# Two DeepNorm layers on one core: the ring of split weights becomes one tile whose four slots start at different distances from multiples of 256 bytes

## The chip, the cores and the metric

The kernel runs on one core of a Trainium2 chip. The metric is the time of one execution on the device, in microseconds (us): lower is better. Before the change it is 847.92 us, the median of 3 runs (846.06 to 848.54).

## The reference, cut to what matters

All arrays are float32; 256 tokens of width 1024 go through two layers. Each layer is a mixer of three branches, fed by one input projection, and a SwiGLU feed-forward part, each followed by a residual and a LayerNorm:

```
for l in range(DEPTH):
    mix = hybrid_mixer(x, w_in[l], attn_sinks[l], conv_w[l], w_branch_a[l], w_branch_b[l], w_branch_c[l], w_out[l])
    x = layer_norm(ALPHA * x + mix, ln1_g[l], ln1_b[l])
    ffn = swiglu(x, w_ffn_gate[l], w_ffn_up[l], w_ffn_down[l])
    x = layer_norm(ALPHA * x + ffn, ln2_g[l], ln2_b[l])
```

The mixer is sliding-window attention with sinks, a gated short convolution, and block attention. Their outputs go through a branch weight each, are gated by a sigmoid and summed, and go through `w_out`. Nearly all arithmetic is in the products of activations with weights.

## The kernel before, in words

**Split operands.** A product is not done in one pass. Every weight block and every activation is split into a high part (rounded to the type fp32r, on ScalarE) and a low part (the float32 value minus the high part, on VectorE), and three matmuls are summed: high by high, high by low, low by high. Where the weights are the stationary operand (lines 366 to 369, `trio`), two matmuls in a row load the same high weights and the third loads the low ones:

```
mm(acc, wh, src[:, 0, :], first, False)
mm(acc, wh, src[:, 1, :], False, False)
mm(acc, wl, src[:, 0, :], False, last)
```

In the helper `tokens` (lines 359 to 364) it is the other way round: the activations are stationary and the weights stream. All these matmuls are issued by line 252, so that in the profile they share that line and are told apart by their tiles: `acc`, `gc`, `br` (stationary weights, 256 columns streamed), `hp` (streamed weights, 256 columns), `pr` and `cv` (streamed weights, 512 columns, in the last projection also 256).

**Pieces, staging and the ring.** The weights come as 140 pieces of 128 x 2048 float32, 70 for each layer, the first of them inside the array `first`. A piece is loaded into one of three `raw` buffers by a DMA from SyncE's queue, split in two chunks of 1024 columns (lines 177 to 181: ScalarE writes `wh`, VectorE writes `wl`), used by TensorE, and dropped. The split parts of a piece lie in a slot. There are four slots (RING), and each has a high and a low tile of 8 KB per partition from a pool of their own (line 122, `wts`; line 172). A few pieces around the feed-forward part go instead into the places `wA` and `wB`, which share memory with other tiles. The tiles of split weights and activations all start at multiples of 256 bytes.

**Addresses of the activations.** The tile `xx` (the layer's input, split) and the tile `y` (the branches' inputs) begin with 48 unused floats (AHEAD, lines 299 and 646), so that every operand read from them starts 192 bytes past a multiple of 256; the tiles `rest` fill the line up. The feed-forward's hidden activations (`hidA`, `hidB`) and the merged branches (`mx`) start at multiples of 256. All blocks of weights and activations that a matmul reads are 512 or 1024 bytes long or apart, so the distance between the starts of its two operands, counted modulo 256 bytes, is the same for all matmuls of one kind.

**What sets the order.** The program is written in a fixed order for TensorE, VectorE, ScalarE and SyncE (line 126). The class `Plan` (lines 53 to 101) keeps estimated times of the engines, and the splits and evictions are put in the order that it finds; `open_splits` (line 159) starts a piece's split as soon as a slot has been dropped. These estimates know nothing of addresses. Between the long streams of matmuls stand small ones: transposes (`tp`, line 265), attention scores (`s`) and attention outputs (`yp`, lines 484 and 486).

Of the kernel before, what the change touches and what calls it, by code (L numbers as in the profile page):

```python
# [10 lines left out]
FR = mybir.dt.float32r  # L11
# [5 lines left out]
P = 128  # L17
# [7 lines left out]
PIECE = 2048  # L25
CHUNK = 1024
RING = 4
# [6 lines left out]
FAR = 1.0e30  # L34
LINE = 64
EARLY = 7
AHEAD = 48


# [77 lines left out]
def trunk(ctx: ExitStack, tc: tile.TileContext, x, first, w, sinks, conv, ln, out):  # L117
    nc = tc.nc
    pool = lambda name, bufs, **k: ctx.enter_context(tc.tile_pool(name=name, bufs=bufs, **k))
    const = pool("const", 1)  # L120
    raws = pool("raws", RAWS)
    wts = pool("wts", RING)
    keep = pool("keep", 1)
    work = pool("work", 2)
    ps = pool("ps", 4, space=bass.MemoryType.PSUM)
    ctx.enter_context(tc.manual_schedule(engines={ENG.PE, ENG.DVE, ENG.Activation, ENG.SP}))
# [8 lines left out]
    total = L * PER_LAYER  # L135
    slots = [0.0] * RING
    spare, ready, chunks, raw, landed, rawfree = {}, {}, {}, {}, {}, {}
    pos = {"load": 0, "split": 0, "take": 0}

    def cut(j):  # L140
# [3 lines left out]
    def load():  # L144
        j = pos["load"]
        if j >= total:
            return
        pos["load"] += 1
        if j:
            raw[j] = raws.tile([P, PIECE], FT, name="raw")  # L150
            for s in cut(j):
                nc.sync.dma_start(raw[j][:, s], w[j - 1][:, s])
        landed[j] = max(landed.get(j - 1, 3.5), rawfree.get(j - RAWS, 0.0) + 2.0) + 3.0
        open_splits()
# [4 lines left out]
    def open_splits():  # L159
        while pos["split"] < pos["load"]:  # L160
            j = pos["split"]
            if j in place:
                if place[j] not in spare:
                    return
                t = spare.pop(place[j])
                both = keep.tile([P, 2, PIECE], FR, tag=place[j], name="w" + place[j])
                ready[j] = both[:, 0, :], both[:, 1, :]
            else:
                if not slots:
                    return  # L170
                t = slots.pop(0)
                ready[j] = wts.tile([P, PIECE], FR, name="wh"), wts.tile([P, PIECE], FR, name="wl")
            pos["split"] += 1
            if j:
                split_piece(j, max(t, landed[j]))
# [7 lines left out]
    def split_piece(j, t, n=CHUNK):  # L183
        def last(task):
            rawfree[j] = task.ready
            load()

        need = T.pe + 5.2 * (j - pos["take"])
        ss = [slice(c, c + n) for c in range(0, PIECE, n)]
        chunks[j] = [T.add(parts(j, s), t - (1.5 if len(cut(j)) > 1 and not i else 0.0), max(need - t, 0.0) + 0.001 * i, last if s.stop == PIECE else None)  # L190
                     for i, s in enumerate(ss)]

    def take():
        j = pos["take"]
        pos["take"] += 1
        T.run()
        T.finish(*chunks.pop(j))
        return j

    def drop(j):  # L200
        if j in place:
            if j % PER_LAYER == N_IN + N_BR + N_OUT:
                spare["B"] = T.pe
        else:
            slots.append(T.pe)
        del ready[j]
        open_splits()
# [90 lines left out]

    xx = keep.tile([P, AHEAD + KD * 2 * S], FR, name="xx")
    xx = xx[:, AHEAD:].rearrange("p (k a s) -> p k a s", k=KD, a=2)  # L300
    xk = [xx[:, k] for k in range(KD)]
    rest = keep.tile([P, LINE - AHEAD], FT, name="rest")
    nc.gpsimd.memset(rest, 0.0)

    both = keep.tile([P, KD, 2 * S], FT, tag="A", name="first")
    rest = keep.tile([P, LINE - AHEAD], FT, name="rest2")
    nc.gpsimd.memset(rest, 0.0)
# [12 lines left out]
    spin = ps.tile([P, P], FT, tag="o", name="spin")  # L320
    for i in range(EARLY):
        nc.tensor.matmul(spin, idle, idle, start=True, stop=True)
# [289 lines left out]
    def mixer_tiles():  # L612
        mix = keep.tile([P, 18 * S + 4 * (S + 2) + 56], FT, tag="mix", name="mix")
        aq, ak, av, cq, ck, cv = [
            mix[:, lo * S:hi * S].rearrange("p (k s) -> p k s", k=k)
            for lo, hi, k in ((0, 4, 4), (4, 5, 1), (5, 6, 2), (6, 10, 4), (10, 14, 4), (14, 18, 2))]
        return aq, ak[:, 0, :], av, cq, ck, cv, mix[:, 18 * S:18 * S + 4 * (S + 2)].rearrange("p (k s) -> p k s", k=4)
# [26 lines left out]
    for l in range(L):  # L644
        aq, ak, av, cq, ck, cv, up = tiles = mix or mixer_tiles()
        y = keep.tile([P, AHEAD + 12 * 2 * S], FR, tag="A", name="y")
        y = y[:, AHEAD:].rearrange("p (b k a s) -> p b k a s", b=3, k=4, a=2)
        nc.gpsimd.memset(up[:, :, 0:2], 0.0)
# [39 lines left out]
        for n in range(2):  # L688
            j = take()
# [120 lines left out]
        merge()  # L810
        spare["A"] = spare["B"] = T.pe
        open_splits()

        hid, last_f = [], {f: [] for f in range(NF)}
# [127 lines left out]
```

## Time and profile before

| what | value |
|---|---|
| median of 3 runs | 847.92 us (846.06 to 848.54) |
| the profiled execution: time, span | 849.0 us, 847.2 us |
| TensorE matmul busy, share of the span | 833.2 us, 98% |
| TensorE weight loads busy | 793.3 us, 94% |
| VectorE, ScalarE, GpSimd busy | 582.7, 456.0, 56.8 us |
| mean granted TensorE clock | 0.996 |
| read from HBM | 153.11 MB, 182 GB/s over the span |

The profile is of one execution. The span runs from its first to its last instruction, and the execution's own time is 1.8 us longer. A matmul's busy time overlaps that of the next, so what a matmul costs in a stream is read from a row of the chain that ended last: its length divided by its number of matmuls. That chain is followed back from the last instruction; a row of it gives start, length, engine, tile written, line and the number of instructions.

### The profile page before, as it was taken

How to read it: one execution, taken by the hardware profiler on the slowest of the kernel's cores; microseconds unless marked ns; L12 is line 12 of the kernel's file. 1: busy time of each engine (PE TensorE's matmuls, PEld its weight loads, DVE VectorE, ACT ScalarE, POOL GpSimd, SP SyncE). 2: the span in 40 equal slices, each digit the busy share in tenths (PEclk: the TensorE clock that was granted, in tenths of full speed). 3: DMA queues.
4: the chain of work that ended last, by engine and by line, in shares of the span. 5: the costliest groups of instructions: out<-in, count | busy, mean ns of one | idle time of the engine just before them, and what ended most of it. 6: DMA issues, size and time to landing. Idle time of an engine off the chain costs nothing.

```text
span 847.2 us, 15506 instructions
## 1 busy us (share of the span) xinstructions
PE 833.2 (98%) x6388; PEld 793.3 (94%) x6388; DVE 582.7 (69%) x978; ACT 456.0 (54%) x809; POOL 56.8 (7%) x81
## 2 busy tenths in 40 slices
PE   7999999999999999999999999999999999999996
PEld 6989999999899999988899899999998999999885
DVE  4688999576967566545657799966688666556435
ACT  5667687645525445434347776865563345444320
POOL 2002500000110000000000044000000100000000
PEclk9999999999999999999999999999999999999999
DMA  8843445555655555556336424554646465545511
GB/s 298 298 167 133 149 154 202 192 200 199 249 199 200 178 176 194 199 190 232 126 106 244 149 100 140 210 205 169 222 165 243 169 226 195 198 172 182 195 50 50
DMA packets 23462, 155.15 MB, mean 183 GB/s; under 512 B 2624, under 2 KB 2912, under 8 KB 5984
## 3 DMA queue, kind: packets, MB, share of 16 engines
q1 hardware_dynamic: 21888, 149.17, 49.9%
q0 software_dynamic: 1216, 4.22, 1.5%
q8 instruction: 50, 0.82, 0.4%
q10 hardware_dynamic: 288, 0.79, 0.3%
q14 instruction: 20, 0.16, 0.1%
HBM read 153.11 MB, written 1.05 MB: 182 GB/s over the span
## 4 chain that ended last, share of the span: by engine, by line
PE 96%; DMA 2%; DVE 1%; ACT 0%; issue 0%; POOLq 0%; POOL 0%; SPq 0%; DVEq 0%
PE acc L252 47%; PE pr L252 17%; PE hp L252 9%; PE br L252 8%; PE gc L252 5%; PE cv L252 3%; PE tp L265 2%; PE s L252 2%; DMA gb<-ln 1%; PE yp L484 1%; DMA first<-first 1%; PE yp L486 0%; DVE xtok L512 0%; DVE wA L181 0%; POOLq L938 0%
## 5 line engine op out<-in xcount | busy, mean ns | idle before, releaser
L252 PE MATMUL acc<-xx,wh 128*128 128x256 f32 x2304 | 405.9, 280 | 4.5 <-ACT wh L270 4.5
L181 DVE TENSOR_TENSOR wl<-raw,wh 128x1024 fp32r<-128x1024 f32 x266 | 322.3, 1229 | 110.1 <-ACT wh L180 109.5
L180 ACT ACTIVATE wh<-raw 128x1024 fp32r<-128x1024 f32 x266 | 274.0, 1053 | 191.9 <-PE acc L252 79.7
L252 PEld LDWEIGHTS acc<-xx,wh 128*128 128x128 f32 x2304 | 351.2, 189 | 5.6 <-ACT wh L270 5.0
L252 PE MATMUL acc<-xx,wl 128*128 128x256 f32 x1152 | 322.1, 280 | 0.2 <-DVE wl L271 0.2
L252 PEld LDWEIGHTS acc<-xx,wl 128*128 128x128 f32 x1152 | 219.3, 190 | 0.6 <-DVE wl L271 0.4
L252 PE MATMUL hp<-wh,xx 128*128 128x256 f32 x384 | 70.4, 281 | 0.0
L277 DVE TENSOR_TENSOR g<-g,acc 128x256 f32<-128x256 f32 x72 | 30.1, 418 | 57.6 <-PE acc L252 57.1
L252 PE MATMUL br<-y,wh 128*128 128x256 f32 x384 | 67.9, 281 | 0.0
L252 PE MATMUL pr<-wh,hidA 128*128 128x512 f32 (+1 forms) x216 | 60.7, 366 | 0.0
L252 PEld LDWEIGHTS hp<-wh,xx 128*128 128x128 f32 x384 | 59.5, 188 | 0.0
L252 PEld LDWEIGHTS br<-y,wh 128*128 128x128 f32 x384 | 58.9, 190 | 0.0
L252 PE MATMUL br<-y,wl 128*128 128x256 f32 x192 | 54.0, 281 | 0.0
L252 PE MATMUL hp<-wl,xx 128*128 128x256 f32 x192 | 53.5, 279 | 0.0
L252 PE MATMUL gc<-xx,wh 128*128 128x256 f32 x256 | 45.3, 281 | 0.0
L252 PEld LDWEIGHTS pr<-wh,hidA 128*128 128x128 f32 x216 | 39.1, 189 | 6.6
L252 PE MATMUL pr<-wh,hidB 128*128 128x512 f32 (+1 forms) x144 | 41.8, 366 | 0.0
L252 PE MATMUL pr<-wl,hidA 128*128 128x512 f32 (+1 forms) x108 | 39.5, 366 | 0.0
L252 PEld LDWEIGHTS gc<-xx,wh 128*128 128x128 f32 x256 | 39.3, 190 | 0.0
L252 PEld LDWEIGHTS hp<-wl,xx 128*128 128x128 f32 x192 | 36.1, 188 | 0.0
L252 PEld LDWEIGHTS br<-y,wl 128*128 128x128 f32 x192 | 36.0, 188 | 0.0
L252 PE MATMUL gc<-xx,wl 128*128 128x256 f32 x128 | 36.0, 281 | 0.0
(133 smaller groups left out, 957.8 us busy)
## 6 DMA issues: line engine op xcount, KB each, us to landing
raw<-w SPq DMA_DIRECT2D x136, 1024.0 KB, 5.0
gb<-ln POOLq DMA_DIRECT2D x8, 512.0 KB, 5.1
raw<-w SPq DMA_DIRECT2D x6, 512.0 KB, 11.3
first<-first SPq DMA_DIRECT2D x2, 512.0 KB, 9.2
xtok<-x SPq DMA_DIRECT2D x2, 512.0 KB, 6.2
out<-xtok SPq DMA_DIRECT2D x3, 256.0 KB, 2.0
first<-first ACTq DMA_DIRECT2D x1, 512.0 KB, 8.6
first<-first ACTq DMA_DIRECT2D x1, 256.0 KB, 4.6
```

The source lines that it names most:

```text
L180: return [act(n) + (lambda: nc.scalar.activation(wh[:, s], raw[j][:, s], AF.Copy),), dve(n) + (lambda: nc.vector.tensor_sub(wl[:, s], raw[ ...
L181: dve(n) + (lambda: nc.vector.tensor_sub(wl[:, s], raw[j][:, s], wh[:, s].bitcast(FT)),)]
L252: nc.tensor.matmul(acc, a, b, start=start, stop=stop)
L265: nc.tensor.transpose(tp[:, i, :], src(i), ident)
L277: return [dve(n) + (lambda: nc.vector.tensor_mul(dst, a, b),)]
L484: nc.tensor.matmul(yp[los[a], :], v[:, 0, vsel[a]], pts[a][:, 0:2, :], start=True, stop=False)
```

## The change

The pool of the ring is gone. One tile `ring` of 16448 floats per partition is taken as the first tile of the pool `keep`, and a slot is a pair of slices of it: the high part of 2048 floats, right behind it the low part. The four slots start at the floats 8, 4112, 8224 and 12344, that is 32, 64 and 128 bytes past and 32 bytes short of a multiple of 256 bytes (the tile itself starts at a multiple). Slots are used in turn. The tile is 256 bytes larger than the eight tiles were, so `xx`, `y` and all else behind it move by 256 bytes and stay where they were modulo 256. The distance between the starts of a matmul's two operands, weights minus activations modulo 256, was 64 bytes for `xx` and `y`; it is now 96, 128, 192 and 32 in the four slots. For `hidA`, `hidB` and `mx` it was 0 and is now 32, 64, 128 and 224. `wA` and `wB` stay as they were.

```
+SLOTS = (8, 4112, 8224, 12344)
+SLOTS_END = 16448
...
-    wts = pool("wts", RING)
     keep = pool("keep", 1)
+    ring = keep.tile([P, SLOTS_END], FR, name="ring")
...
+    turns = [0]
...
-                ready[j] = wts.tile([P, PIECE], FR, name="wh"), wts.tile([P, PIECE], FR, name="wl")
+                ready[j] = [ring[:, lo:lo + PIECE] for lo in (SLOTS[turns[0] % RING], SLOTS[turns[0] % RING] + PIECE)]
+                turns[0] += 1
```

No compute instruction changes its place on any engine. What changes is a part of the waits. A tile of a pool is given out again when everything that read it is done; of a slice, only the readers of the same bytes are waited for. On VectorE, before, in the first projections (`raw` a loaded piece, `wl` and `wh` its low and high part, the names in brackets the semaphores waited for: DMAHW a load, PE a matmul, Activation ScalarE):

```order
L181 TENSOR_TENSOR wl<-raw,wh 128x1024 [waits DMAHW3_49,PE_49,Activation_49]
L181 TENSOR_TENSOR wl<-raw,wh 128x1024 [waits Activation_49]
L181 TENSOR_TENSOR wl<-raw,wh 128x1024 [waits DMAHW4_49,PE_49,Activation_49]
L181 TENSOR_TENSOR wl<-raw,wh 128x1024 [waits Activation_49]
L181 TENSOR_TENSOR wl<-raw,wh 128x1024 [waits DMAHW5_49,Activation_49]
L181 TENSOR_TENSOR wl<-raw,wh 128x1024 [waits Activation_49]
```

The same place on VectorE in the changed kernel, where both parts lie in the tile `ring`:

```order
L186 TENSOR_TENSOR ring<-raw,ring 128x1024 [waits DMAHW3_49,PE_49,Activation_49]
L186 TENSOR_TENSOR ring<-raw,ring 128x1024 [waits PE_49,Activation_49]
L186 TENSOR_TENSOR ring<-raw,ring 128x1024 [waits DMAHW4_49,PE_49,Activation_49]
L186 TENSOR_TENSOR ring<-raw,ring 128x1024 [waits PE_49,Activation_49]
L186 TENSOR_TENSOR ring<-raw,ring 128x1024 [waits DMAHW5_49,Activation_49]
L186 TENSOR_TENSOR ring<-raw,ring 128x1024 [waits Activation_49]
```

No row moved. The wait for TensorE, which stood whole ahead of a piece's first chunk, is now one for the first half of the slot's old content ahead of the first chunk and one for the second half ahead of the second.

## The prediction

> **What bounds the kernel now.** I read the page first: the busy times, the chain by engine, and the costliest groups.
>
> ```profile
> PE 833.2 (98%) x6388; PEld 793.3 (94%) x6388; DVE 582.7 (69%) x978; ACT 456.0 (54%) x809; POOL 56.8 (7%) x81
> PE 96%; DMA 2%; DVE 1%; ACT 0%; issue 0%; POOLq 0%; POOL 0%; SPq 0%; DVEq 0%
> L252 PE MATMUL acc<-xx,wh 128*128 128x256 f32 x2304 | 405.9, 280 | 4.5 <-ACT wh L270 4.5
> L181 DVE TENSOR_TENSOR wl<-raw,wh 128x1024 fp32r<-128x1024 f32 x266 | 322.3, 1229 | 110.1 <-ACT wh L180 109.5
> L180 ACT ACTIVATE wh<-raw 128x1024 fp32r<-128x1024 f32 x266 | 274.0, 1053 | 191.9 <-PE acc L252 79.7
> L252 PE MATMUL acc<-xx,wl 128*128 128x256 f32 x1152 | 322.1, 280 | 0.2 <-DVE wl L271 0.2
> ```
>
> TensorE makes up 96% of the chain. In the largest groups it waits 4.5 us for the first split (line 270, at the start) and 0.2 us for line 271; it never waits for a split of the ring (lines 180 and 181). Those splits wait for each other and for TensorE. So neither loads nor splits bound the kernel. What counts is how fast TensorE takes one matmul after another.
>
> That is not one number. The second view is the chain in order of time (start, length, engine, tile, line, number of matmuls), here its rows of 36 or more 256-column matmuls in the first layer up to the feed-forward part, with two short ones, and the feed-forward part and the last projection of that layer:
>
> ```profile
> 11.66 11.18 PE acc L252 x82
> 22.84 8.17 PE hp L252 x72
> 35.81 10.90 PE acc L252 x96
> 47.41 4.09 PE acc L252 x36
> 64.88 5.47 PE acc L252 x48
> 74.09 8.18 PE acc L252 x72
> 86.01 9.54 PE acc L252 x84
> 100.65 9.54 PE acc L252 x84
> 114.59 8.18 PE acc L252 x72
> 127.87 8.18 PE acc L252 x72
> 139.79 9.54 PE acc L252 x84
> 152.16 5.85 PE acc L252 x48
> 158.01 33.92 PE br L252 x288
> 191.93 22.61 PE gc L252 x192
> 237.24 8.48 PE hp L252 x72
> 249.65 2.83 PE hp L252 x24
> 252.70 5.66 PE hp L252 x48
> 258.57 2.83 PE hp L252 x24
> 261.40 4.10 PE acc L252 x36
> 265.72 97.52 PE acc L252 x828
> 363.24 57.12 PE pr L252 x252
> ```
>
> Divide length by count. 8.18 / 72, 9.54 / 84 and 10.90 / 96 give 113.6 ns for one matmul; 33.92 / 288, 22.61 / 192, 97.52 / 828 and 8.48 / 72 give 117.8. These are the same matmuls, of the same shape, at the same distance of 64 bytes between their two operands, under a granted clock of 1.00 in both places (last view below). So there are two paces, and a stream that has begun in one keeps it: 828 matmuls stay at 117.8, although other engines come and go beside them. What changes the pace is a break: after the scores and transposes of the attention the stream comes back at 113.6, after the break at 152 us at 117.8, and after the two transposes ahead of 261.40 at 113.9 for 36 matmuls, only to go on at 117.8 after the next two. I read this as two streams of reads, the one of the moving operand and the one of the next weights, that stand to each other in one of two phases.
>
> There is a third pace. The end of the last projection in the timeline (start, length, engine), where `hidB` and the weights both begin at multiples of 256 bytes:
>
> ```profile
> 837.24 0.28 PE L252 MATMUL pr<-wh,hidB 128*128 128x256 f32 x1
> 837.36 0.88 PE L252 MATMUL pr<-wB,hidB 128*128 128x256 f32 x6
> 838.08 0.28 PE L252 MATMUL pr<-wh,hidB 128*128 128x256 f32 x1
> ```
>
> From 837.36 to 838.08 there are 6 matmuls: 120 ns each, at distance 0. So the addresses do have a part in it.
>
> **The change, part by part.** First, how many matmuls it touches. The groups of 256 columns on the page:
>
> ```profile
> L252 PE MATMUL hp<-wh,xx 128*128 128x256 f32 x384 | 70.4, 281 | 0.0
> L252 PE MATMUL br<-y,wh 128*128 128x256 f32 x384 | 67.9, 281 | 0.0
> L252 PE MATMUL br<-y,wl 128*128 128x256 f32 x192 | 54.0, 281 | 0.0
> L252 PE MATMUL hp<-wl,xx 128*128 128x256 f32 x192 | 53.5, 279 | 0.0
> L252 PE MATMUL gc<-xx,wh 128*128 128x256 f32 x256 | 45.3, 281 | 0.0
> L252 PE MATMUL gc<-xx,wl 128*128 128x256 f32 x128 | 36.0, 281 | 0.0
> ```
>
> With the two `acc` groups they are 2304 + 1152 + 384 + 384 + 192 + 192 + 256 + 128 = 4992. The rows at 117.8 hold 48 + 288 + 192 + 72 + 24 + 48 + 24 + 828 = 1524 in the first layer (the 48 at 152 us carry a restart in their length, and go on into the 288). The second layer has the same program; I take twice that, 3048 slow matmuls, and 4992 - 3048 = 1944 at 113.6. The mean is (3048 x 117.8 + 1944 x 113.6) / 4992 = 116.2 ns, and the difference of the paces is 4.2 ns.
>
> (a) The distances. The change does not take the two paces away by anything that the trace shows. It does change, at every piece, the distance at which the two streams run: a piece is 48 matmuls, and its successor lies in another slot. So the pace is set anew about every 5.6 us and cannot be carried through 828 matmuls. What it is set to, no row shows for distances of 32, 96 and 128 bytes; at 192 none either, as weights minus activations. Bounds: all 4992 at 113.6 is 3048 x 4.2 = 12.8 us less; all at the 120 of distance 0 is 4992 x 3.8 = 19.0 us more. Between them I take what breaks have done so far. Of the rows above with at least 36 matmuls, those that begin after a break, twelve run at 113.6 to 114 (82, 72, 96, 36, 48, 72, 84, 84, 72, 72, 84 and the 36 at 261.40; the first, with 136, still contains waits of the start, and I count it with its neighbours) and four at 117.8 (48 at 152 us, 72, 48, 828). The 24s are left out, as two transposes part them and they are hardly new beginnings. One new start in four is slow: 4992 / 4 = 1248 slow matmuls in place of 3048, and 1800 x 4.2 = 7.6 us less.
>
> (b) The 512-column matmuls. 57.12 / 252 is 226.7 ns each at distance 0. `cv` at distance 64 is the other row there is:
>
> ```profile
> 51.51 5.49 PE cv L252 x24
> ```
>
> 5.49 / 24 is 228.8. The four projections hold some 800 of them; if all went from the one to the other, it would be 800 x 2.1 = 1.7 us more, and as much less is the bound on the other side. I take nothing, and keep 1.7 both ways.
>
> (c) The finer waits. The first chunk of a piece may be written when half of the slot's old matmuls are done, 24 x 117.8 ns = 2.8 us earlier than now. TensorE waits for no ring split, so this buys nothing; what hides it is the slack of the splits. The added waits on VectorE (one ahead of a second chunk) let nothing through later than before, since TensorE's progress was waited for at the first chunk already. Nothing queued behind them comes later. Cost 0.
>
> (d) ScalarE and VectorE write to starts that are not multiples of 64 bytes in two of the slots. No row shows such a write; below, it cannot gain anything, as both are off the chain. Above: two chunks of a piece take VectorE 2 x 1229 = 2.5 us in a piece's 48 x 117.8 = 5.7 us. In the busiest long stretch, by windows,
>
> ```profile
> 262.00:363.00 101.00, 101.00 (x861) 101.00 (x861) 62.69 (x92) 48.41 (x72) 0.00 (x0) 1.00 0.57 196
> 32.00:152.00 120.00, 119.98 (x998) 113.88 (x996) 100.84 (x219) 87.94 (x207) 19.10 (x20) 1.00 0.50 178
> ```
>
> (columns: PE, PEld, VectorE, ScalarE, GpSimd busy, clock, DMA share, GB/s) VectorE is busy 62.7 of 101 us in the feed-forward part, and 100.8 of 120 in the mixer, which is the place where its cover is thin: 19 us in 120. All of its work there would have to be a fifth slower to matter. Cost 0.
>
> The sum: 7.6 us less. The profiled execution took 849.0 us and would take 841.4. The median of the runs lies 1.1 us below that execution, so I give 847.9 - 7.6 = **840.3 us**.
>
> **The rivals.**
>
> *All fast.* The new distances stay clear of each other and every stream runs at 113.6: 12.8 us less, with the 512-column matmuls perhaps 1.7 more off: 835.1, down to 833.4. For it: a pace of 113.6 is held for 96 matmuls in a row, so it is a steady one. Against it: four different distances would all have to be good.
>
> *Nothing.* The pace is a matter of when the streams start, and addresses only matter at distance 0. A change of slot inside an unbroken stream is then no new start, the 3048 stay slow, and the time stays at 847.9. For it: 828 matmuls pass 17 changes of slot without a change of pace (though all at equal distance). Against it: 120 beside 117.8. The Trainium skill speaks for this rival: its page "SBUF — State Buffer", section "Who interferes with whom", gives TensorE two independent read ports, one for the moving operand and one for the weights, and says that it never waits on anyone. By it all matmuls of one shape would run alike wherever they read; the trace has 113.6, 117.8 and 120, so I give it little.
>
> *Slower.* The new distances include 32 and 96 bytes, which are odd multiples of 32, and 32 is the nearest to 0, the worst that the trace shows. If the two slots that lie 32 bytes off a multiple of 64 run at 120, and the other two as forecast (three in four fast, 114.65), the mean is (120 + 114.65) / 2 = 117.3 against 116.2 now: 4992 x 1.1 = 5.5 us more, 853.4. With all four at 120 it is 866.9. It decides as soon as the mean pace is over 116.2 ns; two slots at 118.5 with two others at 114 still break even. For it: distance 0 has no fast pace at all in the trace. Against it: 64 has.
>
> **How the numbers follow.** A measurement of this kernel can tell about 0.3% from no change: 2.5 us, so faster means below 845.4 and slower above 850.5. Chances: the forecast, one start in four slow, 0.36, of which 0.03 falls within 0.3%; all fast 0.24; nothing 0.12; slower 0.28. Faster is 0.33 + 0.24 = 0.57, the same 0.15, slower 0.28. The range reaches from all fast with a little beyond (833.4, less some 2 us for `hidB`'s 120 and for the rough count: 831) to the slower case with two slots at 120 and the 512-column matmuls against it (853.4 + 1.7, and a part of the way to 866.9: 858). What is left out is the far end of the slower case and a gain beyond the fast pace, under 0.2 together. The forecast's own range is 836 to 845.
>
> **What would show it right or wrong.** Right: in the chain the feed-forward rows of 828 matmuls take about 95 us in place of 97.5, and in the timeline the pace changes from slot to slot, with stretches of 113.6 inside that row; the waits of TensorE stay as they are. All fast: 94.1 us for these 828 and 32.7 for the 288 `br`. Nothing: 97.5 again. Slower: over 98 us there, with paces of 120 and more in single pieces, and rows of the mixer that were at 113.6 above 115. Wrong in another way: waits of TensorE for `ring` at lines 185 and 186, or chunks that take longer than 1229 and 1053 ns by so much that they make it wait.

## The result, and the profile after

The changed kernel takes 857.33 us (median; 856.41 to 857.52, 4 runs) against 847.21 us before (the three runs above and a fourth): a ratio of 1.0118, with a 95% interval of 1.0104 to 1.0132. It is slower, where I had forecast faster.

TensorE is busy with matmuls for 843.4 of the 855.0 us. From the page of the changed kernel, in lines that the prediction showed of the kernel before (`ring` now stands for `wh` and `wl`):

```profile
L257 PE MATMUL acc<-xx,ring 128*128 128x256 f32 x3456 | 418.7, 281 | 2.4 <-ACT ring L275 2.2
L186 DVE TENSOR_TENSOR ring<-raw,ring 128x1024 fp32r<-128x1024 f32 x266 | 322.7, 1229 | 93.2 <-ACT ring L185 92.2
L185 ACT ACTIVATE ring<-raw 128x1024 fp32r<-128x1024 f32 x266 | 274.9, 1054 | 104.6 <-PE pr L257 52.2
```

TensorE waits 2.4 us for the first split (line 275, at the start; it was 4.5, at line 270) and for none at lines 185 and 186, and a chunk takes 1229 ns on VectorE and 1054 on ScalarE, against 1229 and 1053. So neither the waits nor the odd starts of the writes have a part in it. Some rows of the chain in order of time, changed kernel (start, length, engine, tile, line, number):

```profile
33.23 11.43 PE acc L257 x96
72.65 8.50 PE acc L257 x72
84.93 9.96 PE acc L257 x84
152.67 5.85 PE acc L257 x48
...
266.96 97.82 PE acc L257 x828
364.78 58.42 PE pr L257 x252
426.84 8.53 PE hp L257 x72
453.21 11.38 PE acc L257 x96
572.63 5.89 PE acc L257 x48
688.18 97.87 PE acc L257 x828
786.05 61.45 PE pr L257 x330
```

The mixer's rows have lost their fast pace: 8.50 / 72 and 9.96 / 84 are 118.1 and 118.6 ns where 113.6 stood. The rows that were slow got no faster: 97.82 / 828 is 118.1. For the accounting, the same places of the second layer in the chain of the kernel before:

```profile
423.97 8.48 PE hp L252 x72
450.32 10.90 PE acc L252 x96
566.67 5.85 PE acc L252 x48
681.27 97.52 PE acc L252 x828
778.79 60.90 PE pr L252 x330
```

From the row of 96 to the row of 48 the mixer took 116.35 us in either layer (35.81 to 152.16, 450.32 to 566.67) and takes 119.44 and 119.42: 6.2 us more. From there to the 828, 113.56 and 114.60 have become 114.29 and 115.55: 1.7 more. The two rows of 828: 0.3 more each. From the 512-column matmuls of the first feed-forward part to `hp`, 60.73 has become 62.06, 1.3 more, and from those of the second to the end of the span 68.4 has become 69.0, 0.5 more. Together 10.3 us. The start (up to the row of 96) came 2.6 us earlier in this execution, 33.23 against 35.81, so the span grew by 7.8 only, from 847.2 to 855.0. The medians differ by 10.1, as the accounting without the start does.

What each slot costs is read from a view by windows that begin and end with a piece, here four pieces of 48 matmuls in the feed-forward part, in the slots with distances 96, 128, 192 and 32 (window, length, then PE busy; the counts include the neighbours' matmuls at both edges):

```profile
268.21:273.85 5.63, 5.63 (x50) 5.63 (x49) 3.50 (x5) 2.82 (x5) 0.00 (x0) 1.00 0.79 242
273.85:279.55 5.70, 5.70 (x50) 5.70 (x49) 3.50 (x5) 2.70 (x4) 0.00 (x0) 1.00 0.58 198
279.55:285.20 5.65, 5.65 (x50) 5.65 (x49) 3.50 (x5) 2.70 (x4) 0.00 (x0) 1.00 0.51 178
285.20:290.88 5.68, 5.68 (x50) 5.68 (x49) 3.51 (x5) 2.71 (x4) 0.00 (x0) 1.00 0.57 186
```

Divided by 48, the lengths are 117.3, 118.8, 117.7 and 118.3 ns. The pace does change from piece to piece, as I had said, but none of the four is fast.

### The profile page after: what moved, and what is told of

It reads as the page before. It is cut to its first block, busy times and chain, and to the rows that moved or that the text cites. A ratio compares the mean times of both kernels' runs of the same rounds, so it can differ in the third digit from the quotient of the medians.

```text
span 855.0 us, 15528 instructions
## 1 busy us (share of the span) xinstructions
PE 843.4 (99%) x6388; PEld 800.7 (94%) x6388; DVE 585.9 (69%) x978; ACT 458.3 (54%) x809; POOL 56.9 (7%) x81
## 4 chain that ended last, share of the span: by engine, by line
PE 96%; DMA 2%; DVE 1%; ACT 0%; issue 0%; POOLq 0%; SPq 0%; POOL 0%; DVEq 0%
PE acc L257 47%; PE pr L257 18%; PE hp L257 9%; PE br L257 8%; PE gc L257 5%; PE cv L257 3%; PE tp L270 2%; PE s L257 2%; DMA gb<-ln 1%; PE yp L489 1%; DMA first<-first 1%; PE yp L491 0%; DVE xtok L517 0%; DVE wA L186 0%; POOLq L943 0%
## 5 line engine op out<-in xcount | busy, mean ns | idle before, releaser
L257 PE MATMUL acc<-xx,ring 128*128 128x256 f32 x3456 | 418.7, 281 | 2.4 <-ACT ring L275 2.2
L257 PEld LDWEIGHTS acc<-xx,ring 128*128 128x128 f32 x3456 | 412.1, 188 | 4.3 <-ACT ring L275 2.7
L186 DVE TENSOR_TENSOR ring<-raw,ring 128x1024 fp32r<-128x1024 f32 x266 | 322.7, 1229 | 93.2 <-ACT ring L185 92.2
L185 ACT ACTIVATE ring<-raw 128x1024 fp32r<-128x1024 f32 x266 | 274.9, 1054 | 104.6 <-PE pr L257 52.2
L257 PE MATMUL hp<-ring,xx 128*128 128x256 f32 x576 | 70.8, 282 | 0.0
L257 PEld LDWEIGHTS hp<-ring,xx 128*128 128x128 f32 x576 | 68.7, 188 | 0.1
L257 PE MATMUL br<-y,ring 128*128 128x256 f32 x576 | 68.4, 281 | 0.0
L257 PEld LDWEIGHTS br<-y,ring 128*128 128x128 f32 x576 | 68.2, 188 | 0.0
L257 PE MATMUL pr<-ring,hidA 128*128 128x512 f32 (+1 forms) x324 | 67.1, 368 | 0.0
L257 PEld LDWEIGHTS pr<-ring,hidA 128*128 128x128 f32 x324 | 55.8, 188 | 11.0
```

The lines of the kernel that those rows point to most:

```text
L185: return [act(n) + (lambda: nc.scalar.activation(wh[:, s], raw[j][:, s], AF.Copy),), dve(n) + (lambda: nc.vector.tensor_sub(wl[:, s], raw[ ...
L186: dve(n) + (lambda: nc.vector.tensor_sub(wl[:, s], raw[j][:, s], wh[:, s].bitcast(FT)),)]
L257: nc.tensor.matmul(acc, a, b, start=start, stop=stop)
```

## The experiments

**The theories.** A: each distance between the two operands has paces of its own, and 96, 128 and 32 bytes have no fast one. B: the change of distance inside a stream breaks the fast phase, whatever the distances. C: the one tile and its other waits cost the time. A further question is whether the two paces at one distance really are two phases, and whether a break chooses between them.

**All slots at multiples of 256 (u000).** One tile, but the old distances.

```
-SLOTS = (8, 4112, 8224, 12344)
+SLOTS = (0, 4096, 8192, 12288)
```

> The ring is one tile as in the changed kernel, but all four slots start at multiples of 256 bytes, so that every distance is that of the kernel before. Theory A (each distance between weights and activations has paces of its own, and only at 64 bytes is 113.4 ns one of them): 847 us, the 828 matmuls of the feed-forward part at 117.8 ns, mixer rows at 113.6. Theory B (the change of distance from slot to slot breaks the fast phase, whatever the distances): 847 us as well, since nothing changes from slot to slot. Theory C (one tile in place of eight, with its other waits, costs the time): 857 us.

847.27 us, ratio to the kernel before 1.0003 (0.9993 to 1.0014). Here and below a ratio is to executions of the kernel before that were taken beside the run (medians of 846.3 to 846.8 us). From its chain:

```profile
137.62 9.54 PE acc L257 x84
263.55 97.52 PE acc L257 x828
```

Both rows have the length of before, to the hundredth. Theory C falls.

**All slots at one distance: 128 (u064), 192 (u128), 96 (u032), 32 (u224), 0 (u192), 160 (u096).** The same edit, with all four slots 64, 128, 32, 224, 192 or 96 bytes past a multiple of 256, for example u064:

```
+SLOTS = (16, 4112, 8208, 12304)
```

> All four slots 64 bytes past a multiple of 256: distance 128 to the split activations everywhere, no change from slot to slot. In the changed kernel stationary weights at this distance took 118.7 ns on average. Theory A: 118.7 everywhere with 256 columns, also in the mixer: some 860 us. Theory B: the stream finds a steady phase and the mixer is back at 113.6 ns: 848 us or less.

> All four slots 128 bytes past: distance 192 everywhere. In the changed kernel stationary weights took 117.8 ns there and streamed weights (hp) 114.0. Theory A: 117.8 in all streams with stationary weights, 114 in hp, 512-column matmuls at 232 to 233: about 855 us. Theory B: mixer rows at 113.6, hp at 113.4 as well: 843 to 848 us.

> All four slots 32 bytes past: distance 96 everywhere. In the changed kernel stationary weights took 118.2 ns there, streamed weights 119.9, 512-column matmuls 233 to 234. Theory A: these numbers everywhere, about 861 us. Theory B: mixer rows at 113.6 again, 848 us or less.

> All four slots 32 bytes short of a multiple of 256: distance 32 everywhere, the last of the changed kernel's four. There stationary weights took 118.3 ns at it. Distances with paces of their own: 118.3 or more in all streams, no row at 113.6, 512-column matmuls at 233: 858 to 861 us. A change from slot to slot to blame: mixer rows at 113.6, 848 us.

> All four slots 192 bytes past a multiple of 256, as the activations are: distance 0 for them. If distance decides, 120.0 ns with stationary weights in every stream (as the last projection's 256-column matmuls on hidB at distance 0 in the kernel before), and 227 ns for the 512 columns of cv: some 866 us. If the multiple of 256 made the 120 there, something else.

> All four slots 96 bytes past a multiple of 256: distance 160 everywhere, untried so far. What the other runs have shown: with stationary weights a fast pace of 113.4 ns exists at 64 and 192, the odd multiples of 64; 0, 32, 96 and 128 have none. If that holds as a rule, 160 has none either: 118 to 119 ns in every stream and 857 to 862 us. If the fast pace is a matter of being far from 0, as 160 is, mixer rows at 113.4 and 850 us or less.

From the chains, a row of the mixer and the row of 828 of each; first distance 128 (u064):

```profile
141.94 10.08 PE acc L257 x84
270.09 98.25 PE acc L257 x828
```

Distance 192 (u128), with a row of the second layer:

```profile
140.73 9.89 PE acc L257 x84
266.99 97.52 PE acc L257 x828
452.62 10.89 PE acc L257 x96
```

Distance 96 (u032):

```profile
141.37 9.97 PE acc L257 x84
268.51 99.36 PE acc L257 x828
```

Distance 32 (u224):

```profile
142.05 9.94 PE acc L257 x84
269.41 97.98 PE acc L257 x828
```

Distance 0 (u192):

```profile
142.09 10.07 PE acc L257 x84
270.73 99.35 PE acc L257 x828
```

Distance 160 (u096):

```profile
141.87 10.07 PE acc L257 x84
270.29 99.36 PE acc L257 x828
```

| distance | time, us | ratio to before (95%) | ns in the mixer row | ns in the row of 828 |
|---|---|---|---|---|
| 0 | 865.47 (one run) | | 119.9 | 120.0 |
| 32 | 858.10 | 1.0142 (1.0124 to 1.0160) | 118.3 | 118.3 |
| 64 (u000) | 847.27 | 1.0003 (0.9993 to 1.0014) | 113.6 | 117.8 |
| 96 | 859.94 | 1.0159 (1.0138 to 1.0180) | 118.7 | 120.0 |
| 128 | 860.72 | 1.0170 (1.0150 to 1.0190) | 120.0 | 118.7 |
| 160 | 865.88 | 1.0227 (1.0210 to 1.0244) | 119.9 | 120.0 |
| 192 | 853.08 | 1.0074 (1.0052 to 1.0097) | 117.7 | 117.8 |

No slot changes its distance in these kernels, and still 0, 32, 96, 128 and 160 have no row at 113.6 (u128's other rows of 72 and 84 are as slow as the one shown, but its 10.89 / 96 is 113.4: at 192 the fast pace exists). Theory B would have given 848 in each. The changed kernel's 857.33 lies among its four distances' 859.94, 860.72, 853.08 and 858.10, whose mean is 857.96. Theory A stands. For 160 I had expected 857 to 862 us and 118 to 119 ns; no fast pace came, as expected, but the rows are at 119.9 and 120.0, as slow as at distance 0.

**Everything moved by 64 bytes (both64).** Slots 64 bytes past a multiple of 256, activations at a multiple.

```
-SLOTS = (8, 4112, 8224, 12344)
+SLOTS = (16, 4112, 8208, 12304)
...
-AHEAD = 48
+AHEAD = 0
```

> One tile, all four slots 64 bytes past a multiple of 256, and the unused floats ahead of xx and y taken away, so that these start at a multiple of 256: every operand has moved by 64 bytes, and the distance is 64 again. If the distance decides: mixer rows at 113.6 ns and the 828 matmuls of the feed-forward part at 117.8 as in the kernel before, some 847 to 850 us (the 512-column matmuls on hidA, hidB and mx go from distance 0 to 64, 227 to 229.5 ns, and the few pieces in wA and wB from 64 to 0). If the slots' own place in the memory decides: the paces of the run with all slots at 64 bytes, 118.7 to 120 ns, some 860 us.

842.84 us, ratio 0.9963 (0.9950 to 0.9976). From its chain:

```profile
112.54 8.18 PE acc L257 x72
125.83 8.48 PE acc L257 x72
264.64 93.88 PE acc L257 x828
```

The fast pace is back (8.18 / 72 is 113.6), in slots whose place alone had given 120. And at distance 64 there are rows at 113.6 with the operands in either place (u000, both64). So it is the distance that decides, not the place. It is also faster than I expected: 93.88 / 828 is 113.4, the whole feed-forward part of the first layer in the fast pace, while a row of the mixer (8.48 / 72) has gone over to the slow one. The same distance, the same breaks, but other phases after them; some matmuls ahead of the breaks did have another distance than before (those with `wA` and `wB`, and those on `hidA`, `hidB` and `mx`), but no run shows that this is why.

**A scan of breaks (kickscan).** The kernel before, with transposes of the identity, read by nobody, put between blocks of the feed-forward part.

```
+KICKS = ({6: 1, 8: 2, 10: 3, 12: 4, 14: 5, 16: 6}, {6: 6, 8: 5, 10: 4, 12: 3, 14: 2, 16: 1})
...
+    def kick(n):
+        for lo in range(0, n, 3):
+            tp, _ = bank([P, 3, P], "o", "kick")
+            for i in range(min(3, n - lo)):
+                nc.tensor.transpose(tp[:, i, :], ident, ident)
...
         for f in range(4, NF):
+            kick((KICKS[l]).get(f, 0))
```

> The kernel before, all at distance 64, with breaks put into the feed-forward part: 1 to 6 transposes of the identity, that nobody reads, ahead of every second block from the seventh on (1, 2, 3, 4, 5, 6 in the first layer, 6 to 1 in the second). If the two paces are two phases of the same stream, the pace after a break is a matter of its length: some of the 96-matmul stretches behind the breaks run at 113.4 ns and some at 117.8, each steadily up to the next break. If the pace belongs to the stage (other engines, data, the weights' loads), all of them stay at 117.8. The breaks cost 42 transposes of 109 ns, 4.6 us, and a start each; the time itself is no matter.

One run took 847.52 us. The chain of its first layer's feed-forward part from the 2 transposes on, and behind it two stretches of the second layer, after 4 and after 2:

```profile
282.96 11.31 PE acc L253 x96
294.27 0.33 PE kick L274 x3
294.60 10.90 PE acc L253 x96
305.50 0.44 PE kick L274 x4
305.94 11.31 PE acc L253 x96
317.25 0.55 PE kick L274 x5
317.79 10.90 PE acc L253 x96
328.69 0.66 PE kick L274 x6
329.35 33.93 PE acc L253 x288
...
711.24 10.90 PE acc L253 x96
733.60 10.92 PE acc L253 x96
```

10.90 / 96 is 113.5 and 11.31 / 96 is 117.8. After 2 transposes slow, after 3 fast, after 4 slow, after 5 fast, after 6 slow, each until the next break; the instructions of VectorE and ScalarE come in the order of the kernel before. In the second layer, with the numbers in reverse, it is slow after 6 and fast after 5, and then stays fast after 4, 3, 2 and 1 (10.90 and 10.92 above). So the pace does not belong to the stage or to the other engines. It is a state that a stream keeps and that a break can turn over; to which side, the number of transposes does not say, not even together with the pace ahead of them: 4 after a fast stretch led to slow in the first layer and left the second fast. What else counts is open. I went on with 5, which led from slow to fast both times.

**Breaks where the slow streams begin (kick5, and after_kick5 on the changed kernel).** `kick(5)` at two places of each layer:

```
+        kick(5)
         for b in range(3):
             branch(b)
...
         for f in range(4, NF):
+            if f == 5:
+                kick(5)
```

> The kernel before (distance 64) with a break of 5 transposes of the identity, read by nobody, at two places of each layer: ahead of the first branch, and ahead of the sixth block of the feed-forward part. In the scan of breaks 5 transposes led from 117.8 to 113.4 ns both times. If the phase theory holds at these places: 780 matmuls of the feed-forward part (3.4 us) and the 480 of branches and last gate (2.1 us) run at 113.4 in each layer, 11 us less, against some 3 us for the breaks: 838 to 839 us. If the phase after a break cannot be steered like this: no row changes its pace, and the breaks make it 849 us.

> The changed kernel with the same breaks at the same places. If the distances 96, 128 and 32 have no fast phase, no break can lead into one: the rows keep their 118 ns, and the breaks add 3 us: 860 us. If the changed kernel merely came out of its breaks in bad phases, the 828 and 480 matmuls get faster here too, and it takes 849 us or so.

kick5 takes 837.29 us, ratio 0.9894 (0.9872 to 0.9916). Its feed-forward part in the chain:

```profile
266.57 0.55 PE kick L273 x5
267.11 92.49 PE acc L252 x816
```

92.49 / 816 is 113.3, so the whole part now runs in the fast pace, 816 matmuls that took 117.8 each before. The branches behind the other break did the same: 32.66 / 288 is 113.4 in the chain, where 33.92 / 288 stood. after_kick5 takes 858.80 us, ratio 1.0143 (1.0125 to 1.0162), more than the 1.0118 without breaks. The same part of its chain:

```profile
270.34 96.47 PE acc L257 x816
```

96.47 / 816 is 118.2. These breaks found no fast phase to lead into, as theory A has it.

**Two distances that both have a fast pace, in turn (alt).**

```
-SLOTS = (8, 4112, 8224, 12344)
+SLOTS = (0, 4128, 8192, 12320)
```

> One tile, slots at 0, 128, 0 and 128 bytes past multiples of 256: the distance changes at every piece between 64 and 192, which alone have shown a pace of 113.4 ns with stationary weights. If a change of distance inside a stream does no harm by itself: rows of the mixer at 113.6 remain, and the time lies between the two uniform kernels or below, 845 to 853 us. If the change from slot to slot breaks the fast phase by itself: no row of the mixer below 116 ns, 855 us or more.

840.57 us, ratio 0.9928 (0.9913 to 0.9944), better than I had expected and better than either distance alone (847.27 and 853.08). The rows of 828 and of `br` in its chain:

```profile
157.32 32.85 PE br L257 x288
263.58 93.91 PE acc L257 x828
675.73 94.12 PE acc L257 x828
```

93.91 / 828 is 113.4, 94.12 / 828 is 113.7 and 32.85 / 288 is 114.1. With the same breaks ahead of them, the uniform kernels at 64 and 192 both had 97.52 there. Where the pace turns over is seen by windows over single pieces. In the second layer's 828, the piece of 48 that begins 12 matmuls in, at distance 192, and the next, at 64:

```profile
677.11:682.76 5.65, 5.65 (x50) 5.65 (x49) 3.50 (x5) 2.84 (x5) 0.00 (x0) 1.00 0.81 252
682.76:688.20 5.44, 5.44 (x50) 5.44 (x49) 3.51 (x5) 2.71 (x4) 0.00 (x0) 1.00 0.52 184
```

That is 117.7 and 113.3 ns, without a break between them, and all pieces behind them keep the 113.3. In the first layer the 12 matmuls ahead of the first change, at distance 192, take 117.6, and from the next piece on, at 64, it is fast. So a change of slot can lead a slow stream into the fast pace, and here it did, in the long streams of both layers. It need not: the change from 64 to 192 after the first 12 of the second layer left the stream slow, and some rows of that layer's mixer are slow that were fast before (8.48 / 72). Why the fast pace is kept through some 15 later changes of slot is not explained by these runs.

## Why the prediction was wrong

- **What bounds the kernel, and the two paces:** right. TensorE's pace decides, and the scan of breaks shows that the paces of 113.4 and 117.8 ns are states of one stream. u000 shows that the tile and its waits cost nothing, as (c) had it, and the chunks' 1229 and 1054 ns, where 1229 and 1053 stood, confirm (d).
- **The step that failed** is the sum of (a): "One new start in four is slow". It took how often the streams had come back fast at distance 64 for a law of all distances. I had written that no row shows the paces at 32, 96 and 128 bytes, and then put the price of 64 on them. The uniform kernels give 118.3 at 32, 117.3 to 120.0 at 96 and 118.6 to 120.0 at 128, without any fast pace; only at 192 is there one. In place of 7.6 us less, the stretches of 256-column matmuls brought some 8 us more, most of it in the mixer, which had been fast and could only lose. The median still lies inside the range of 831 to 858, but in the end of it that was kept for the slower rival; the forecast's own range ended at 845.
- **That a change of slot is a new start:** right in part. In `alt`, with 64 and 192, a change of slot led both long streams from slow to fast, and the time fell by 5.8 us (0.7%), where I had given 7.6 to the change. But the pace was not drawn anew at each piece, one in four slow: once fast, the streams stayed so to their end. That the sum of (a) would have come near for these distances is luck.
- **(b), the 512-column matmuls:** the term was larger than its bound of 1.7 us. 58.42 / 252 is 231.8 ns where 226.7 stood at distance 0, and the two projections from there on make up 1.8 us by themselves. Counted from start to start in both traces, the 512-column matmuls of `pr` and `cv` took 3.3 us more. The bound came from 228.8 at distance 64, and no row had the new distances.
- **Two readings of the trace that I had wrong,** neither with a change of sign. The 36 matmuls at 261.40 do not come after transposes: the `hp` row ahead of them ends there (258.57 + 2.83 is 261.40), so the pace turned where the weights became the stationary operand, without a break. And the second layer is not twice the first: its `hp` rows from 423.97 on (8.48 / 72, then two of 5.66 / 48) are slow at 117.8. With them and two rows of 24 that I left out, some 3260 matmuls were slow, not 3048, and counted as in (a) over both layers 11 of 33 starts, not one in four.
- **The rivals:** "slower" was right in its sign, at 0.28, and its mechanism was near: new distances behave like 0. Its price came from two slots at 120; in truth all four gave 117.3 to 118.8. Of its signs, mixer rows above 115 came (118.1 and 118.6), over 98 us for the 828 (97.82) and pieces at 120 did not. The break-even that I named, a mean pace of 116.2, was passed by every slot. "All fast" and "nothing" are both off. Behind "nothing" stood the Trainium skill (the page "SBUF — State Buffer", section "Who interferes with whom"), which calls TensorE's two read ports independent and says that it never waits on anyone. That section is about engines that run at once; my step from it, that all matmuls of one shape run alike wherever they read, does not agree with these runs: with the same instructions, distances alone make 847.27 or 865.88 us. The measurement decides.

What the two phases are inside the chip stays open. A collision of the two read streams is what I argued from, and no run shows it directly.

## What to carry to other kernels

Where a chain's rows give the same matmul different costs, divide length by count for every row before anything else: it shows whether a stream has several steady paces, and breaks between streams may be a cheap handle on them (kick5: 9 us for 20 transposes). When operands are moved in memory, measure one uniform kernel for each distance first; the paces at one distance say nothing of those at another. Count what is already good, since a change to all matmuls can take it away: here about a third of the 256-column matmuls were fast, and they were most of the loss.

## What the runs showed of the hardware

- For matmuls of 256 fp32r columns with a 128 x 128 weight load each, the distance of the two operands' starts modulo 256 bytes sets the pace: 113.4 or 117.8 ns at 64 and at 192, 117.3 to 120.0 at 0, 32, 96, 128 and 160 (runs with all slots at one distance; row means).
- At a distance with two paces the state is kept for hundreds of matmuls (816 at 113.3, 828 at 117.8) and is changed by a break as short as 3 transposes (kickscan, 0.33 us). In `alt` it turned from 117.7 to 113.3 at a change of distance from 192 to 64 without a break.
- With 512 columns, 226.7 ns at distance 0 was the best seen (57.12 / 252); the mixed distances of the changed kernel took 231.8.
